# Weight loads of a hybrid encoder layer: issued from GpSimd's queue in place of SyncE's

## The chip, the core and the metric

The kernel runs on one core of a Trainium2 chip. TensorE multiplies matrices, VectorE and ScalarE do elementwise work, GpSimd can do some of it too, and SyncE (SP) computes nothing: it issues transfers. A transfer is issued by one engine's queue and then carried by the core's 16 DMA engines, which move it between the main memory and the on-chip memory; an engine that needs it waits for its landing. The metric is the device time in microseconds, lower is better. The kernel before took 2712.67 us (median of three runs, 2711.59 to 2713.68).

## What is computed

One layer of a bidirectional encoder, for a prompt of 1024 tokens and a sample of 2048, each with 16 learned meta tokens ahead, width 1024, in float32. One projection feeds two branches, which are gated, projected, merged and projected again:

```
xn = rmsnorm(h, g_pre)
proj = xn @ w_in + b_in                                  # 1024 -> 6672 columns
na_q, na_k, na_v, na_z, ml_qk, ml_v, ml_z, ml_o, ml_g, mg = split(proj)
ya = (neighbourhood_attention(na_q, na_k, na_v) * silu(na_z)) @ w_a
yb = (mlstm_bidirectional(ml_qk, ml_v, ml_g, ml_o) * silu(ml_z)) @ w_b
ga, gb = split(sigmoid(mg))
y = (ga * ya + gb * yb) @ w_out
out = h + rmsnorm(y, g_post)
```

## The kernel before

**Precision.** Every large product is made of three matmuls: a float32 operand is split into a high part (what the fast matmul format holds) and a low part (the rest), and hi*hi, hi*lo and lo*hi are added (`mm3`). So each weight tile exists twice on the chip, as `whi` and `wlo`, 128 x 1024 or 128 x 1056 numbers each, 512 or 528 KB.

**Where a weight comes from.** `requests` writes down at the start, in order, every weight unit that the dense work will take. A unit comes in one of three ways.
- Raw, the first time it is used: `wload` loads it from the input `wu` into `wraw` (L274); ScalarE copies it to `whi` (L303), VectorE takes the difference for `wlo` (L304), and both halves are written back to main memory to be kept (`wflush`, L331).
- Kept halves: later uses load `wh` and `wl` straight into `whi` and `wlo` (L296).
- Block sums: a part of the input projection uses a Strassen-like scheme with seven products for eight. Its sums of weight blocks are made on the side (`wprep`, `nprep`), stored as `q...`, and loaded in pairs into `whi` and `wlo` (L289).

**Buffers.** There are four `whi` and four `wlo` (`NBW = 4`) and two to four `wraw`. `wtake` hands a unit to the matmuls; `wdone` after a unit's last matmul is followed by `wpump`, which asks for the next load. On the chip that load waits until the buffer's last reader is through, and the matmuls wait until it has landed.

**The two streams.** `dense` runs the projections, the merges and the output products group by group in the order of `PLAN`; `sparse` runs the mLSTM and the attention. `run` weaves the two together by estimated costs. TensorE's order is the order in which this weave writes it down (`manual_schedule` holds TensorE alone). The order of the other engines' instructions, SyncE's and GpSimd's queues among them, is laid out when the program is built, by a simulation with estimated durations; each queue then runs strictly in that order, and an instruction whose wait isn't over holds up those behind it.

**The queues.** SyncE issues nearly every transfer: weights, tokens, the stores of the projections (`st`, `stT`) and their loads by the sparse stream (`raw`, `va`, `um`, `kf`, `tog`), the attention's operands, the kept halves, the gates `tg` and the output. GpSimd's queue holds 100 instructions: small memsets (among them the edges of `raw`, L1413 and L1415, and `st`, L1559), eight small copies, and 14 loads of constants for the attention, one-hot rows (L1096) and masks (L1183).

Of the kernel before, what the change touches and what calls it, by code (L numbers as in the profile page):

```python
# [10 lines left out]
F32 = mybir.dt.float32  # L11
# [126 lines left out]
class K:  # L138
# [127 lines left out]
    def wload(self, most=2):  # L266

        while self.wreq and sum(x[1] is not None for x in self.wraw) < most:
            key, src, nk, w = self.wreq.popleft()
            raw = None  # L270
            if key[0] != "q" and key not in self.wseen:
                self.wseen.add(key)
                raw = self.wrp[0].tile([P, 4 * WU], F32, name="wraw", bufs=self.wrp[1])
                self.nc.sync.dma_start(raw[:, :nk * w], src)  # L274
            self.wraw.append((key, raw, nk, w))

    def wpump(self, most=NBW, parts=1, copy=None):


        nc, wp = self.nc, self.wp  # L280
        self.wload()
        while self.wraw and self.wout < most:
            key, raw, nk, w = self.wraw.popleft()
            n = nk * w
            hi = wp.tile([P, 4 * WU], F32R, name="whi", bufs=NBW)
            lo = wp.tile([P, 4 * WU], F32R, name="wlo", bufs=NBW)
            if key[0] == "q":
                for x, k in zip((hi, lo), key[1:]):
                    nc.sync.dma_start(x[:, :n].bitcast(F32), self.qd[k][:, :])  # L289
                self.wrdy.append([x[:, :n].rearrange("p (h k c) -> p h k c", h=2, k=4) for x in (hi, lo)])  # L290
                self.wout += 1
                self.wload()
                continue
            if raw is None:
                for x, d in zip((hi, lo), self.wkept[key]):
                    nc.sync.dma_start(x[:, :n].bitcast(F32), d[:, :])  # L296
            else:
                for a in range(parts):
                    c = slice(a * n // parts, (a + 1) * n // parts)
                    if copy:  # L300
                        copy(hi[:, c], raw[:, c])
                    else:
                        nc.scalar.activation(hi[:, c], raw[:, c], AF.Copy)  # L303
                    nc.vector.tensor_tensor(lo[:, c], raw[:, c], hi[:, c].bitcast(F32), op=ALU.subtract)  # L304
                if key[1] in N_COLS and key[0] == "i":
                    j = N_COLS.index(key[1])
                    for a in range(2):
                        d = self.qd[j // 2, f"{j % 2 + 1}{a + 1}"] = self.dp.tile([P, D], F32, name=f"q{j}{a}")
                        for h, x in enumerate((hi, lo)):
                            self.hold.append((d[:, 512 * h:512 * h + 512], x[:, 512 * a:512 * a + 512].bitcast(F32)))  # L310
                else:
                    self.wkept[key] = []
                for x, part in ((hi, "h"), (lo, "l")) if key in self.wkept else ():
                    d = self.dp.tile([P, n], F32, name=f"w{part}{len(self.wkept)}")
                    self.hold.append((d, x[:, :n].bitcast(F32)))
                    self.wkept[key].append(d)
                if not self.early:
                    self.wflush()
                if key[0] in "mo":
                    self.wrdy.append(None)  # L320
                    self.wout += 1
                    self.wload()
                    continue
            self.wrdy.append([x[:, :n].rearrange("p (k c) -> p k c", k=nk) for x in (hi, lo)])
            self.wout += 1
            self.wload()
# [1836 lines left out]
```

## Time and profile before

| | |
|---|---|
| median of the runs | 2712.67 us |
| the profiled execution | 2707.9 us |
| its span, first to last instruction | 2706.1 us |
| instructions | 47482 |
| mean granted TensorE clock | 0.992 |
| moved by DMA | 805.75 MB, mean 298 GB/s |

The profile is of one execution. Its page gives the busy time of each engine (a matmul's end is modelled, so a busy TensorE need not run at its peak), the span in 40 slices, the DMA queues (q1 is SyncE's, q0 GpSimd's), and the chain of work that ended last, followed back from the end. Other views give the waits of one engine by what ended them, the busy time in chosen stretches, and the instructions of a queue in order of time. PE stands for TensorE, DVE for VectorE, ACT for ScalarE, POOL for GpSimd, SPq for SyncE's queue. L274 is line 274 of the kernel.

### The profile page before, as it was taken

The numbers are of one execution on the slowest core, as the hardware profiler recorded it, in microseconds if no ns is written. First come the engines' busy times: TensorE is split into PE (matmuls) and PEld (weight loads), VectorE is DVE, ScalarE is ACT, GpSimd is POOL, SyncE is SP. The second block draws the span as 40 slices with busy tenths as digits, with TensorE's granted clock in tenths as the row PEclk, the third lists the DMA queues.
The fourth block names the chain that finished last, engine by engine and source line by source line (L and its number), as shares of the span: only waits on it lengthen the run. The fifth ranks groups of instructions, "written<-read, shape, count | busy, mean of one in ns | idle before, by whom it ended". The sixth has DMA issues, their size and how long they took to land.

```text
span 2706.1 us, 47482 instructions
## 1 busy us (share of the span) xinstructions
PE 2647.0 (98%) x15928; PEld 2336.6 (86%) x15928; DVE 1943.8 (72%) x5266; ACT 1439.9 (53%) x3388; POOL 16.2 (1%) x100
## 2 busy tenths in 40 slices
PE   9999899998999999999999999999999999999998
PEld 7998798898987999887888888888889998989888
DVE  5655588787766888545686776867478989898954
ACT  5433456554444655555665566656365666656521
POOL 0000000000000000000000000000000000000000
PEclk9999899998999999999999999999999999999999
DMA  9899886899978899878889998899899898898965
GB/s 366 336 342 335 309 306 233 299 336 327 348 228 285 294 320 314 274 265 276 259 271 332 370 297 264 279 331 363 274 305 314 259 309 278 282 305 260 324 238 203
DMA packets 411651, 805.75 MB, mean 298 GB/s; under 512 B 52016, under 2 KB 180992, under 8 KB 409104
## 3 DMA queue, kind: packets, MB, share of 16 engines
q1 hardware_dynamic: 410288, 800.04, 87.9%
q0 software_dynamic: 1120, 2.69, 0.4%
q8 instruction: 126, 2.06, 0.3%
q14 instruction: 117, 0.96, 0.1%
HBM read 548.96 MB, written 253.60 MB: 297 GB/s over the span
## 4 chain that ended last, share of the span: by engine, by line
PE 82%; DMA 9%; DVE 5%; ACT 2%; issue 1%; SPq 1%; DVEq 0%; ACTq 0%
PE pj L202 9%; PE pj L204 9%; PE pj L203 9%; PE pj L971 7%; PE pj L973 7%; PE pj L972 7%; PE pj L776 4%; PE pj L777 4%; PE pj L778 4%; PE pj L1918 3%; PE pj L1919 3%; PE pj L1920 3%; PE sm L1266 3%; PE tr L1251 2%; DMA wraw<-wu 2%
## 5 line engine op out<-in xcount | busy, mean ns | idle before, releaser
L202 PE MATMUL pj<-xh,whi 128*128 128x512 f32 (+1 forms) x896 | 345.5, 386 | 1.0 <-ACT whi L303 0.9
L204 PE MATMUL pj<-xh,wlo 128*128 128x512 f32 (+1 forms) x896 | 337.4, 377 | 5.7 <-DMA wlo<-wl 5.4
L203 PE MATMUL pj<-xl,whi 128*128 128x512 f32 (+1 forms) x896 | 337.9, 377 | 0.1
L776 PE MATMUL pj<-whi,xh 128*128 128x256 f32 (+1 forms) x1152 | 330.9, 287 | 6.8 <-DMA whi<-wh 6.8
L777 PE MATMUL pj<-wlo,xh 128*128 128x256 f32 (+1 forms) x1152 | 326.2, 283 | 3.7 <-DMA wlo<-wl 3.7
L778 PE MATMUL pj<-whi,xl 128*128 128x256 f32 (+1 forms) x1152 | 325.9, 283 | 0.0
L776 PEld LDWEIGHTS pj<-whi,xh 128*128 128x128 f32 x1152 | 218.6, 190 | 7.4 <-DMA whi<-wh 7.0
L777 PEld LDWEIGHTS pj<-wlo,xh 128*128 128x128 f32 x1152 | 218.3, 190 | 4.1 <-DMA wlo<-wl 4.0
L1918 PE MATMUL pj<-whi,mh 128*128 128x256 f32 x768 | 219.8, 286 | 0.5 <-DMA whi<-wh 0.5
L778 PEld LDWEIGHTS pj<-whi,xl 128*128 128x128 f32 x1152 | 218.3, 189 | 0.0
L1920 PE MATMUL pj<-whi,mlo 128*128 128x256 f32 x768 | 216.6, 282 | 0.0
L1919 PE MATMUL pj<-wlo,mh 128*128 128x256 f32 x768 | 216.6, 282 | 0.0
L204 PEld LDWEIGHTS pj<-xh,wlo 128*128 128x128 f32 x896 | 170.9, 191 | 38.8 <-DMA wlo<-wl 6.2
L202 PEld LDWEIGHTS pj<-xh,whi 128*128 128x128 f32 x896 | 170.9, 191 | 30.8 <-ACT whi L303 1.8
L203 PEld LDWEIGHTS pj<-xl,whi 128*128 128x128 f32 x896 | 170.9, 191 | 27.5 <-issue 1.0
L1258 DVE TENSOR_TENSOR pts<-tr,pts 96x384 fp32r<-96x384 f32 (+2 forms) x192 | 118.5, 617 | 57.2 <-ACT pts L1253 55.3
L1253 ACT ACTIVATE pts<-tr 96x384 fp32r<-96x384 f32 (+2 forms) x192 | 103.5, 539 | 98.8 <-PE tr L1251 98.1
L202 PE MATMUL pj<-yh,whi 128*128 128x512 f32 x384 | 154.4, 402 | 0.0
L203 PE MATMUL pj<-yl,whi 128*128 128x512 f32 x384 | 150.9, 393 | 0.8 <-DVE yl L1820 0.8
L204 PE MATMUL pj<-yh,wlo 128*128 128x512 f32 x384 | 151.1, 394 | 0.0
L1918 PEld LDWEIGHTS pj<-whi,mh 128*128 128x128 f32 x768 | 145.4, 189 | 1.5 <-DMA whi<-wh 0.7
L1919 PEld LDWEIGHTS pj<-wlo,mh 128*128 128x128 f32 x768 | 145.5, 189 | 0.8
(368 smaller groups left out, 6962.5 us busy)
## 6 DMA issues: line engine op xcount, KB each, us to landing
whi<-wh SPq DMA_DIRECT2D x136, 512.0 KB
wlo<-wl SPq DMA_DIRECT2D x136, 512.0 KB
whi<-q SPq DMA_DIRECT2D x62, 512.0 KB
wlo<-q SPq DMA_DIRECT2D x50, 512.0 KB
wraw<-wu SPq DMA_DIRECT2D x48, 512.0 KB
gt<-st SPq DMA_DIRECT2D x96, 256.0 KB
tg<-gt SPq DMA_DIRECT2D x96, 256.0 KB
wh<-whi SPq DMA_DIRECT2D x36, 512.0 KB
```

Of the source, the lines that this page charges most:

```text
L202: mm(out, ah, bh, start=start, stop=False)
L203: mm(out, ah, bl, start=False, stop=False)
L204: mm(out, al, bh, start=False, stop=stop)
L776: nc.tensor.matmul(o, xh, wh, start=k == 0, stop=False)
L777: nc.tensor.matmul(o, xh, wl, start=False, stop=False)
L778: nc.tensor.matmul(o, xl, wh, start=False, stop=k == KT - 1)
L971: mm(bank, w[:, 0, k], xh[:, k], start=fresh and k == 0, stop=False, skip_group_check=True)
L972: mm(bank, w[:, 0, k], xl[:, k], start=False, stop=False, skip_group_check=True)
L973: mm(bank, w[:, 1, k], xh[:, k], start=False, stop=k == 3, skip_group_check=True)
L1918: nc.tensor.matmul(o, mh[:, k, xs], wh, start=clear > 0 and k == 0, stop=False)
L1919: nc.tensor.matmul(o, mh[:, k, xs], wl, start=False, stop=False)
L1920: nc.tensor.matmul(o, ml[:, k, xs], wh, start=False, stop=clear < 2 and k == KT - 1)
```

## The change

The three places in which the kernel loads weights issue from GpSimd instead of SyncE. Sources, destinations, sizes, buffers and the order of requests in the code stay.

```diff
@@ wload @@
-                self.nc.sync.dma_start(raw[:, :nk * w], src)
+                self.nc.gpsimd.dma_start(raw[:, :nk * w], src)
@@ wpump @@
             if key[0] == "q":
                 for x, k in zip((hi, lo), key[1:]):
-                    nc.sync.dma_start(x[:, :n].bitcast(F32), self.qd[k][:, :])
+                    nc.gpsimd.dma_start(x[:, :n].bitcast(F32), self.qd[k][:, :])
...
             if raw is None:
                 for x, d in zip((hi, lo), self.wkept[key]):
-                    nc.sync.dma_start(x[:, :n].bitcast(F32), d[:, :])
+                    nc.gpsimd.dma_start(x[:, :n].bitcast(F32), d[:, :])
```

The write-back of the halves (L331), the loads of raw weights for the block sums (L576, L608) and everything else stay with SyncE.

## The prediction

> **What bounds the kernel now.** I read the page first, then TensorE's own waits, then the stretches in which it waits, then the queue that issues the loads.
>
> ```profile
> span 2706.1 us, 47482 instructions
> PE 2647.0 (98%) x15928; PEld 2336.6 (86%) x15928; DVE 1943.8 (72%) x5266; ACT 1439.9 (53%) x3388; POOL 16.2 (1%) x100
> ...
> DMA  9899886899978899878889998899899898898965
> ...
> q1 hardware_dynamic: 410288, 800.04, 87.9%
> q0 software_dynamic: 1120, 2.69, 0.4%
> ...
> PE 82%; DMA 9%; DVE 5%; ACT 2%; issue 1%; SPq 1%; DVEq 0%; ACTq 0%
> ```
>
> TensorE is the bound: busy 2647.0 of 2706.1 us, so all its idle time together is 59.1 us and nothing done to loads can win much more than that. The second thing to see is the DMA row: the 16 DMA engines are nearly full almost everywhere. GpSimd is free (16.2 us busy).
>
> TensorE's waits say how much of the 59.1 us belongs to weights:
>
> ```profile
> PE tr L1539 <- DVE kf L1503: 11.7, 2, 8.9
> PE pj L776 <- DMA whi<-wh: 6.8, 1, 6.8
> PE sm L204 <- DVE ktl L1543: 6.4, 6, 2.8
> PE pj L204 <- DMA wlo<-wl: 5.4, 2, 2.8
> ...
> PE pj L777 <- DMA wlo<-wl: 3.7, 1, 3.7
> ...
> PE pj L202 <- ACT whi L303: 0.9, 1, 0.9
> ...
> PE pj L1918 <- DMA whi<-wh: 0.5, 1, 0.5
> ```
>
> (Total us, times, longest.) Waits for a weight load's landing: 6.8 + 5.4 + 3.7 + 0.5 = 16.4 us, in five events. They cost more than their idle time, as the stretches around them show (the number after POOL's count is the granted TensorE clock, then DMA share and GB/s):
>
> ```profile
> 630.60:642.00 11.40, 0.91 (x5) 0.41 (x3) 1.23 (x2) 0.80 (x3) 0.00 (x0) 0.65 1.01 344
> 642.00:648.00 6.00, 6.00 (x29) 6.00 (x30) 1.99 (x7) 2.60 (x6) 0.00 (x0) 0.52 1.02 368
> 754.00:766.00 12.00, 9.47 (x35) 7.21 (x35) 5.74 (x19) 4.64 (x14) 0.00 (x0) 0.86 0.85 268
> 812.00:824.00 12.00, 9.17 (x32) 6.55 (x31) 3.77 (x16) 1.86 (x4) 0.00 (x0) 0.86 1.03 404
> 900.00:1000.00 100.00, 99.23 (x775) 96.75 (x774) 80.75 (x197) 57.42 (x123) 0.00 (x0) 1.00 1.00 332
> 1500.00:1600.00 100.00, 98.57 (x505) 83.03 (x504) 79.02 (x292) 62.46 (x169) 0.20 (x2) 1.00 0.99 344
> 1800.00:1900.00 100.00, 96.92 (x483) 80.28 (x483) 70.04 (x236) 57.44 (x157) 0.10 (x1) 1.00 1.00 365
> ```
>
> After the stall that ends at 642 TensorE is busy without a gap for 6 us at a granted clock of 0.52: 6 x 0.48 = 2.9 us lost. The stalls near 760 and 817 lose 12 x 0.14 = 1.7 us each. So the weight stalls cost 16.4 + 6.3 = 22.7 us.
>
> Why are those loads late? SyncE's issues before the stall at 760, and pieces of the chain of waits (start, length from issue to landing):
>
> ```profile
> 749.84 0.42 SPq L296 DMA_DIRECT2D whi<-wh  x1
> 750.42 3.92 SPq L835 DMA_DIRECT2D nv<-stT  x6
> 755.36 0.33 SPq L296 DMA_DIRECT2D wlo<-wl  x1
> ...
> 758.19 0.39 SPq L296 DMA_DIRECT2D whi<-wh  x1
> ```
>
> ```profile
> 635.84 6.11 DMA wlo<-wl
> ...
> 755.36 4.79 DMA wlo<-wl
> ...
> 803.13 14.04 DMA wlo<-wl
> ```
>
> The two halves of one weight are 5.5 us apart, because six stores of nv stand between them in SyncE's order. The load itself then took only 4.79 us: it was issued late. The third one, issued at 803.13, took 14.04 us: it was slow, with DMA at 1.03 of its share in that stretch.
>
> SyncE also waits for transfers that its next load doesn't need, and its order is met late where an engine is late:
>
> ```profile
> SPq L2007 <- DVE yo L2006: 40.5, 28, 10.8
> ...
> SPq L1603 <- DMA yb<-szg: 25.9, 12, 3.8
> ```
>
> **The change part by part.** Moved are the raw loads at L274, the block sums at L289 and the kept halves at L296:
>
> ```profile
> L274 SPq DMA_DIRECT2D wraw<-wu x52: 328/494/1561, 2.6 to 946.7; - x52
> ...
> L296 SPq DMA_DIRECT2D whi<-wh x144: 319/378/1519, 461.5 to 2674.3; - x144
> L296 SPq DMA_DIRECT2D wlo<-wl x144: 319/370/1559, 465.3 to 2673.9; - x144
> ```
>
> With the 120 pairs of block sums that the order of the Strassen-like products asks for in the code, that is 52 + 288 + 240 = 580 loads of 512 or 528 KB, about 300 MB of the 800.04 MB. No byte, matmul or wait for data is added; TensorE's order is fixed by hand.
>
> *Loads no longer stand behind stores.* This removes the stalls at 637, 642 and 760, and the 0.5 us. The stall at 817 was a slow transfer in a full stretch; a queue of its own may or may not help, so I count half of its 2.7 + 1.7 us. Sum: 22.7 - 2.2 = **-20.5 us**; bounds 0 and -22.7.
>
> *The price of an issue on GpSimd and the landing.* The trace has no weight load there; the nearest row is the masks' load, 64 partitions of up to 4 KB instead of 128:
>
> ```profile
> L1183 POOL DMA_DIRECT2D kx<-masks x10: 509/513/779, 802.6 to 2423.7; - x10
> ...
> DMA to landing us min/median/max: 3.3/6.7/9.8
> ```
>
> At 0.513 us, 580 issues are 298 us of GpSimd, spread over the span; if the price goes with partitions, 595 us. Both lie beside TensorE. A pair takes 1.0 to 2.1 us. How much time is there? In the last stage loads are issued one weight apart:
>
> ```profile
> 2668.14 0.32 SPq L296 DMA_DIRECT2D wlo<-wl  x1
> ...
> 2673.88 0.32 SPq L296 DMA_DIRECT2D wlo<-wl  x1
> ```
>
> 5.74 us per weight; four buffers, so a load that goes out when its buffer comes free has three more weights ahead of it, 17.2 us. Less 1.0 for the pair and 6.7 for landing, 9.5 us are left; with the largest values (2.1, 9.8), 5.3. So this costs nothing, except where fewer weights are ahead, at the very end, where the row L1918 waits already: I take **+0.3** (2 x 0.513 against 0.32 + 0.38 of the issues there), at most +5.0 (9.8 against 4.79 to land).
>
> The Trainium skill, "SBUF — State Buffer", section "SBUF: two separate sides", speaks against the change: GpSimd writes descriptors through a port pair that VectorE locks in its two-port modes; its next section gives a transfer of about 0.62 us that then took about 3.1. By that page, an estimate of 2.5 us per load would leave 7.0 of the 9.5 us, and the sum would rise only at the end of the kernel, by 2.5. By the row, the ten mask issues stayed within 509 to 779 ns though VectorE was 72% busy; I go by the row.
>
> *Loads now stand behind GpSimd's own instructions.* Those wait long:
>
> ```profile
> POOL kx L1183 <- PE sm L1220: 720.6, 6, 297.0
> POOL raw L1413 <- DVE cv L1428: 273.2, 5, 74.9
> ```
>
> Most of that is GpSimd with nothing else to do. The order on each queue is laid out at build time by estimated times, so a load is late only by what an engine is late against the estimate. SyncE's order is made in the same way, and its longest wait for an engine is 10.8 us (L2007); 9.5 us are covered, 1.3 not. I take **+1**; lower bound 0, upper bound in the rivals.
>
> *SyncE is freed* of 580 issues at about 0.37 us, 215 us, and of waiting for weight buffers. The waits of TensorE for kf and ktl (11.7 and 6.4) end on VectorE, whose inputs come over that queue; I take **-1**, bounds 0 and -18.1. *The order on VectorE, ScalarE and SyncE* is laid out anew with it, and TensorE's waits for them could shrink or grow: **+2**, bounds -10 and +15, the latter near all that TensorE now waits for kf and ktl.
>
> Sum: -20.5 + 0.3 + 1 - 1 + 2 = -18.2 us. The profiled execution took 2707.9 us (span 2706.1 and 1.8 around it), so 2689.7; the median of the runs is 4.8 above that execution, so the forecast is 2712.67 - 18.2 = **2694.5**.
>
> **The rivals.**
>
> *The stalls stay (about 2711).* For it: in three of the four stall rows the DMA share is over 1.00, so the load may be slow on any queue, as the one of 14.04 us was. Against it: 749.84 to 755.36 is pure order, at a share of 0.85. The half hidden gain of one late pair leaves 2.7 + 1.7 at 760 and little else.
> The Trainium skill, "DMA: Bandwidth & Descriptors", section "Issuing engines are not separate DMA queues", says that more issuing engines save issue time alone, which would be this rival.
>
> *Slower: GpSimd's transfers cost the DMA engines more.* q0 uses 0.4 points for 2.69 MB, 0.149 per MB; q1 87.9 for 800.04, 0.110. That is 1.35 times (1.18 to 1.52 with the rounding of 0.4). The moved bytes are 38% of all, so a stretch at full share gets 0.38 x 0.35 = 13% longer. Over the three stretches above, +40 us, with the gain 2694.5 + 40 = 2734. It decides from 0.38 x 300 x excess = 18 us, a price 16% up. Against it: half of q0's loads are under 4 KB per row and write 64 partitions, and their times hold waiting for others.
>
> *Slower: GpSimd's order holds loads up.* A memset of raw or a mask load whose partner is late by more than 9.5 us stops all four buffers; each event costs about 3 us and 1.7 of clock. Four of them eat the gain; ten, +47, give 2741. For it: waits of 75 and 297 us stand in the rows. Against it: SyncE's 10.8.
>
> *Slower: the new order.* Taken at +33 in place of +2 (TensorE's waits for kf and ktl tripled): 2726.
>
> **How the numbers follow.** Under 0.2% (5.4 us) nothing can be told from no change. Forecast 0.56, its own range 2672 (all weight stalls and the kf and ktl waits gone) to 2707; stalls stay 0.14; dearer transfers 0.12; GpSimd's order 0.12; new order 0.06. Faster: 0.53 of the forecast and 0.04 of the stay, 0.57. Same: 0.03, 0.10 and 0.01 each of the two slow rivals, 0.15. Slower: 0.28. The range cuts the lower end where kf's wait, VectorE's own work, would have to go too, and holds the first two slow rivals' low part: 2678 to 2735.
>
> **What would show it.** Right: no wait of TensorE for whi or wlo near 640 and 760, clock 1.00 there, GpSimd's issues at 0.5 to 1.1 us, its landings under 10 us. Wrong: TensorE waiting for whi or wlo in new places with a GpSimd instruction in front (its order), DMA share at 1.00 over most slices with fewer GB/s (dearer transfers), or the same stalls under GpSimd's queue (they stay).

## The result: slower, and the profile after

| | before | after |
|---|---|---|
| median of the runs | 2712.78 us | 2734.36 us |
| lowest to highest | 2711.59 to 2713.68 | 2731.27 to 2736.21 |
| profiled execution, its span | 2707.9, 2706.1 us | 2731.3, 2729.5 us |

The ratio is 1.0079, 95% interval 1.0061 to 1.0096: 21.6 us slower, where the prediction said 18.2 faster. (The kernel before ran once more beside the change, so its median is 2712.78 here.) The page of the kernel after, first its busy times, the DMA row, the two queues, the chain's shares by engine and two rows of DMA issues (the last number is the median from issue to landing):

```profile
span 2729.5 us, 47658 instructions
PE 2653.3 (97%) x15928; PEld 2338.2 (86%) x15928; DVE 1940.8 (71%) x5266; ACT 1440.7 (53%) x3388; POOL 325.9 (12%) x680
...
DMA  9889986799968999988899998898989898898965
...
q1 hardware_dynamic: 326768, 495.58, 54.2%
q0 software_dynamic: 84640, 307.14, 33.7%
...
PE 76%; DMA 14%; DVE 5%; ACT 2%; issue 1%; SPq 1%; DVEq 0%; POOL 0%; ACTq 0%
...
whi<-wh POOLq DMA_DIRECT2D x136, 512.0 KB, 7.3
wlo<-wl POOLq DMA_DIRECT2D x136, 512.0 KB, 7.7
```

The change did what it says: 304 MB went over to q0. TensorE has the same 15928 matmuls in the same order; it was busy 6.3 us longer (its mean granted clock was 0.990 in place of 0.992) and idle 76.2 us in place of 59.1, together the 23.4 us by which the span grew. The two queues' shares are 54.2 + 33.7 = 87.9 and were 87.9 + 0.4. The chain's part in DMA rose from 9 to 14%. TensorE's waits say which transfers these are:

```profile
PE tr L1539 <- DVE kf L1503: 11.1, 2, 6.6
PE sm L204 <- DVE ktl L1543: 9.2, 6, 5.4
PE pj L203 <- DMA xl<-xl: 7.4, 2, 4.1
PE pj L971 <- ACT pj L1010: 6.6, 2, 5.6
PE sc L1668 <- DVE q L1622: 5.6, 1, 5.6
...
PE pj L202 <- ACT xh L389: 2.9, 1, 2.9
...
PE pj L1918 <- DMA whi<-wh: 1.2, 1, 1.2
```

Of the 16.4 us of waits for weights 1.2 are left. The new waits are for tiles that SyncE still loads, or that VectorE and ScalarE make from them.

One place shows how. There both kernels' SyncE reaches the same four loads of 1 MB (`xl`, `xh`, L936) at the same time, 1457.6 us. SyncE's issues (start, length) before:

```profile
1457.61 0.37 SPq L936 DMA_DIRECT2D xl<-xl  x1
1458.07 2.66 SPq L936 DMA_DIRECT2D xh<-xh  x2
1460.78 1.10 SPq L936 DMA_DIRECT2D xl<-xl  x1
1461.93 2.73 SPq L289 DMA_DIRECT2D whi<-q  x1
```

and after, on SyncE and then on GpSimd:

```profile
1457.67 0.37 SPq L936 DMA_DIRECT2D xl<-xl  x1
1458.13 1.44 SPq L936 DMA_DIRECT2D xh<-xh  x2
1459.62 6.71 SPq L936 DMA_DIRECT2D xl<-xl  x1
1466.42 2.31 SPq L712 DMA_DIRECT2D gt<-st  x1
```

```profile
1458.16 0.53 POOL L289 DMA_DIRECT2D whi<-q  x1 [2.46 <-PE sm L203]
1461.88 0.53 POOL L289 DMA_DIRECT2D wlo<-q  x1 [3.18 <-PE pj L973]
```

Before, the next weight stood behind the fourth of these loads. After, two weights set out among them. What both queues moved in the 20 us from 1457.6, before and then after (packets, MB, share of the 16 engines):

```profile
DMA packets 4007, 7.39 MB, mean 369 GB/s; under 512 B 265, under 2 KB 1247, under 8 KB 4006
q1 hardware_dynamic: 4006, 7.37, 103.3%
```

```profile
DMA packets 3111, 7.23 MB, mean 362 GB/s; under 512 B 178, under 2 KB 434, under 8 KB 3110
q1 hardware_dynamic: 2312, 4.27, 64.1%
q0 software_dynamic: 798, 2.94, 38.8%
```

The sum hardly changes; SyncE's queue gets 4.27 MB of it. Before, weights were among its 7.37 MB too, but the four loads came first. In the chain of waits of the kernel after (start, us from issue to landing) that fourth load is the longest transfer; it and two more of the long ones:

```profile
1459.62 23.24 DMA xl<-xl
1534.77 17.31 DMA xh<-t0h
1809.39 17.12 DMA kf<-kf
```

By its semaphore's update in the trace the same load took 12.4 us before (1460.78 to 1473.22).

### The profile page after: what moved, and what is told of

Read it like the earlier page. It is cut to its first block, busy times and chain, and to the rows that moved or that the text cites. A ratio compares the mean times of both kernels' runs of the same rounds, so it can differ in the third digit from the quotient of the medians.

```text
span 2729.5 us, 47658 instructions
## 1 busy us (share of the span) xinstructions
PE 2653.3 (97%) x15928; PEld 2338.2 (86%) x15928; DVE 1940.8 (71%) x5266; ACT 1440.7 (53%) x3388; POOL 325.9 (12%) x680
## 3 DMA queue, kind: packets, MB, share of 16 engines
q1 hardware_dynamic: 326768, 495.58, 54.2%
q0 software_dynamic: 84640, 307.14, 33.7%
## 4 chain that ended last, share of the span: by engine, by line
PE 76%; DMA 14%; DVE 5%; ACT 2%; issue 1%; SPq 1%; DVEq 0%; POOL 0%; ACTq 0%
PE pj L202 8%; PE pj L203 8%; PE pj L204 8%; PE pj L971 7%; PE pj L973 7%; PE pj L972 7%; PE pj L776 4%; PE pj L778 4%; PE pj L777 4%; PE pj L1918 3%; PE pj L1919 3%; PE pj L1920 3%; PE sm L1266 2%; PE tr L1251 2%; DMA stk<-nq 2%
## 5 line engine op out<-in xcount | busy, mean ns | idle before, releaser
L1918 PE MATMUL pj<-whi,mh 128*128 128x256 f32 x768 | 219.2, 285 | 1.2 <-DMA whi<-wh 1.2
L1918 PEld LDWEIGHTS pj<-whi,mh 128*128 128x128 f32 x768 | 145.1, 189 | 2.2 <-DMA whi<-wh 1.4
```

Source lines behind the costliest of these rows:

```text
L1918: nc.tensor.matmul(o, mh[:, k, xs], wh, start=clear > 0 and k == 0, stop=False)
```

## The experiments

Three theories. **S**, sharing: the 16 DMA engines serve both queues at once, so weights that have time to spare take turns from SyncE's loads that have none. **O**, order: the build lays out the other engines' instructions anew, and that order is worse. **D**, dearer: GpSimd's issues or transfers cost more in themselves.

To tell O apart, most kernels here hold VectorE, ScalarE and SyncE to the exact order of the kernel before, with order-only links between neighbours on an engine that make no engine wait for another. The loads that change queue (`off`) are left out of the links:

```diff
+        row = [row[n] for n in order]
+        for a, b in zip(row, row[1:]):
+            tc.add_manual_dep(b, a.name, info, reason="pin")
...
-        K(tc, ins, outs).run(ctx)
+        k = K(tc, ins, outs)
+        k.run(ctx)
+        pin(tc, k.off)
```

Line numbers in their profiles lie 1 to 6 higher. As TensorE's order is the same in all kernels, the n-th matmul of one trace can be put beside the n-th of the kernel before, and the difference of their starts is TensorE's lag. The table under e13 gives how much the lag grew in each stretch.

**e1: all weights on GpSimd, every other order as before.**

```diff
-                self.nc.sync.dma_start(raw[:, :nk * w], src)
+                self.off.add(self.nc.gpsimd.dma_start(raw[:, :nk * w], src).ins.name)
...
```

(and the same at L289 and L296)

> Weights on GpSimd as in the change, but the instructions of VectorE, ScalarE and SyncE (its other transfers) are held in exactly the order that they have in the kernel before. Theory S (sharing: a queue of its own gives the weight loads, which have time, an equal turn at the 16 DMA engines with SyncE's loads, which have none): the loss stays, 2728 to 2740 us, with no wait of TensorE for whi or wlo over 1 us but waits that end on SyncE's loads. Theory O (order: the build laid out the other engines anew and worse): the loss goes and the weight stalls' 20 us come in, 2690 to 2707 us. Theory D (GpSimd's transfers or issues cost more in themselves): as S, 2728 to 2740.

Measured: 2741.84, ratio 1.0110 (1.0089 to 1.0131): 1.8 us over the range that S and D share, and far from O's. The longest wait for a weight's landing is 1.2 us, at the kernel's end; at the opening TensorE waits 3.0 us for a raw weight's split on ScalarE, which S did not name.

**e2: the weights back on SyncE, the other engines in the order of the changed kernel.**

> The mirror image: weights back on SyncE, in the order that the build of the change gives to VectorE, ScalarE and SyncE's other transfers. S and D: near the kernel before, 2706 to 2722 us. O: as slow as the change, 2728 to 2740 us.

Measured: 2714.81, ratio 1.0009 (0.9998 to 1.0020). The loss is there without the new order, and the new order without the queue has no loss that can be measured. O falls.

**e3: as e1, each load in two halves of its columns, to make packets half as long.**

```diff
-                    nc.sync.dma_start(x[:, :n].bitcast(F32), d[:, :])
+                    for c in range(2):
+                        c = slice(c * n // 2, (c + 1) * n // 2)
+                        self.off.add(nc.gpsimd.dma_start(x[:, c].bitcast(F32), d[:, c]).ins.name)
```

> As the first, but each weight load is cut into two of half the columns, so rows of 2 KB in place of 4 KB and 1160 issues on GpSimd in place of 580. S, if turns are taken by packet: the weights' share falls, SyncE's loads land sooner (tg's median, 8.4 us in the change, under 7.8), 2715 to 2728 us. O: the same as the first run within 3 us. D: dearer, over 2738 us.

Measured: 2745.94, ratio 1.0116 (1.0093 to 1.0140). It didn't test what it was made for: q0 still shows 71808 packets of 4096 bytes, two rows of 2 KB in each. As a test of D it says something: its time is in D's range (over 2738), but so is e1's, and 580 more issues than e1 moved the ratio from 1.0110 to 1.0116, well inside the intervals.

**e4, e6, e7: one kind of load alone on GpSimd**, the 52 raw ones (L274), the 288 kept halves (L296), the 240 block sums (L289).

> Only the 52 raw loads on GpSimd, all other orders as before. S: the start loses what it lost in the change (TensorE's start held up by xt, some 4 to 8 us) and little else, 2714 to 2724 us. O: at or under the kernel before, 2700 to 2713. D: 52 issues cost next to nothing, 2711 to 2716.

> Only the 288 loads of kept halves on GpSimd (most of them issued at 400 to 1100 us and from 1950 on), the other 292 on SyncE, the order of VectorE, ScalarE and SyncE that of before. Theory S: only those steps of e1 remain at whose time kept halves are under way: +6 at 482, -11.5 at 638, +6 at 669 to 690, -7 at 760 to 821, +6.5 at 1034 to 1079, +7 at 1958 to 2050; none at the opening nor at 1269 to 1815. Sum about +7: 2714 to 2726. Theory D: each load costs its share wherever it is, 288/580 of the losses of e1 (about 48) less the gains (18): 2712 to 2724 as well, but with small steps also after 2050, where e1 showed none.

> Only the 240 loads of block sums on GpSimd (all issued at 1100 to 1950 us), the other 340 on SyncE, the order of VectorE, ScalarE and SyncE that of before. Theory S: only the losses of e1 at 1269 to 1302 (5.8), 1478 (5.7), 1815 (6.7) and part of 1958 (up to 4.4) remain, and the stalls for weights of before at 638 to 821 come back, so that no gain is left: 2728 to 2738, slower than before by about 20. Theory D: 240/580 of the losses: as much, but spread over the stretch and not at these four places.

Measured: 2719.16, ratio 1.0024 (1.0012 to 1.0037); 2719.66, 1.0021 (1.0009 to 1.0033); 2734.26, 1.0081 (1.0065 to 1.0096). The three add up to 1.26%, near e1's 1.10%. e4's time is in S's range and above those of O and D, and it lost 5.1 us at the opening, as S named; e6's is in both S's and D's. e7's is in S's range, and it lost at places that S named (6.1 us near 1478, 3.4 at 1815, 7.0 near 1958) and at one that it didn't (3.5 at 1873), while 1302 stayed small; it is flat after 1970. Its 3.8 us at 1000 to 1110 come before its first moved load (1126 us); e4 shows 3.6 there after its last (953 us). e6 has the gains, and steps at 482, 650 to 715 and 1034 to 1079, but only 2.1 of the 7 us that S put at 1958 to 2050. It also lost 6.0 us after 2200, where e1 lost 0.8; S has no step there, and D's many small ones don't fit either: most of it is one, at 2226. The trace shows there a load of SyncE's (`vr`) that took 15.5 us (9.0 before), and a wait of 3.5 us for what is made from it: the kind of step that S means, at a place that it did not name.

**e5: as e1, but 524 loads of weights wait until the SyncE load that stood just ahead of them before has landed.**

```diff
+    for i, j in json.loads(zlib.decompress(base64.b85decode(AFTER))):
+        tc.add_manual_dep(w[i], sp[j].name, info, reason="after")
```

(here the link is a wait for the landing; `w` are the weights' loads, `sp` SyncE's)

> All 580 loads of weights on GpSimd and VectorE, ScalarE and SyncE held to the order of the kernel before, as in e1, with one thing added: 524 of the 580 loads of weights wait until the one load of SyncE's that stood just ahead of them in the kernel before has landed (the other 56, whose tile would by the trace of before be late by it, don't wait). So a load of weights no longer shares the 16 DMA engines with the loads that were issued ahead of it. By the landings of before this starts a weight 3.3 us later in the median, and none of the 524 lands under 3 us ahead of its first use. Theory S (the weights' own queue takes turns from SyncE's tight loads): the losses of e1 against before (TensorE fell back by 2.9 us at 7 to 14, 6.2 at 482, 6.2 at 669 to 690, 6.5 at 1034 to 1079, 5.8 at 1269 to 1302, 5.7 at 1478, 6.7 at 1815, 7.2 at 1958 to 2050) go in the main, and the gain at 638 to 646 and 760 to 821 (-18) stays: 2690 to 2718. Theory D (an issue or a transfer by GpSimd is dearer or disturbs SyncE's queue in itself): the waits take no issue and no transfer away, so 2735 to 2755.

Measured: 2720.90, ratio 1.0032 (1.0019 to 1.0044). With every one of GpSimd's 580 issues still made, 21 of e1's 30 us are gone. D can't explain that; S had it at 2718 at most, so a little is missing. Two places say why. One is that of the four loads: e5's DMA in the 20 us from their first issue, and the issue of the fourth:

```profile
q1 hardware_dynamic: 2029, 3.84, 52.2%
q0 software_dynamic: 1008, 3.67, 48.3%
```

```profile
1448.95 5.54 SPq L937 DMA_DIRECT2D xl<-xl  x1
```

Here the waits only pushed weights back from the loads ahead into these four: q0 moved 3.67 MB beside them, more than in the changed kernel, and this step stayed (4.4 us). The other lies after 2200, where e5 fell back by 8.3 us and e1 by 0.8: there TensorE waits for weights that GpSimd issued late, two of them after pauses of 14 and 15 us (e1's longest between 2190 and 2500 is 8.1).

```profile
PE pj L1919 <- DMA whi<-wh: 4.5, 3, 2.2
PE pj L1920 <- DMA wlo<-wl: 1.8, 2, 0.9
```

**e8, e10, e11: other tenants for GpSimd's queue.** In e8 542 stores move to it (`st`, `stT`, kept halves), weights stay on SyncE and nothing is held. In e10 the tight loads move, `kf` (L1585), `um` (L1591), `va` (L1476), `raw` (L1416) and `xl`, `xh` (L936); in e11 only `kf`, `um`, `xl`, `xh`; VectorE and ScalarE are held.

```diff
-        nc.sync.dma_start(um, src)
+        self.off.add(nc.gpsimd.dma_start(um, src).ins.name)
```

> The opposite way to give SyncE's queue room: the weights stay on SyncE and 542 stores of SBUF tiles to DRAM (kept halves, features, keys, gates, values) are issued by GpSimd; nothing is held, so the order of the other engines may change a little. Theory S: stores on a queue of their own take turns from the tight loads as well, while SyncE's loads no longer stand behind stores that wait for their data; both signs: 2700 to 2735, and the transfers of xl, kf, um are longer while a store is under way. Theory D: 542 issues by GpSimd against 580 in the change: slower by about 20.

> The mirror image: the weights stay on SyncE, and 368 loads that TensorE, VectorE or ScalarE use soon after they land (kf, um, va, the raw keys and queries, and xl and xh of L936) are issued by GpSimd; VectorE and ScalarE are held to the order of before, SyncE's order may change. Theory S: now these loads take their turns beside the queue of weights and stores instead of standing behind it, and land earlier, while the weights have 16.5 us to spare in the median: 2688 to 2714. If both queues share alike whoever is in them, but GpSimd's order holds a load up behind another's buffer: up to 2730. Theory D (GpSimd's loads are dearer in themselves): 368/580 of e1's 48 us of losses, and on loads without slack: 2735 to 2760.

> As e10 with 160 loads only: kf (L1585), um (L1591), and xl and xh of L936 on GpSimd; va and the raw keys and queries stay on SyncE. Theory S: the steps of e1 at 669 to 690, 1269 to 1302, 1478 and 1815 were these tiles, so most of e10's gain is in these: 2692 to 2714. Theory D: 160/580 of 48 us on loads without slack: 2722 to 2735.

Measured: e8 2724.20, ratio 1.0039 (1.0026 to 1.0052); e10 2727.57, 1.0060 (1.0046 to 1.0073); e11 2711.74, 0.9995 (0.9984 to 1.0007). e8 lost 6.0 us at 1440 to 1520 without a weight on GpSimd, but not at the four loads: by its semaphore the fourth landed 14.2 us after its issue (12.4 before), and TensorE did not wait for it. It waited 2.8 us for keys made from `kf`, which took 12.7 us to land (8.2 before). In those 13 us GpSimd's stores moved 0.79 MB and SyncE's queue 4.39; as SyncE's order is not held in e8, this fits S without showing it. e8's time is in S's wide range; of the 20 us that D gave it, it lost 11. e10 missed S's gain and came near the end that S gave to GpSimd's order; D's 2735 and more is missed too, and e11 missed D's 2722 by far; it is inside S's range, without a gain that can be measured. What GpSimd waited for in e10, issuing one load behind another's buffer:

```profile
POOL um L1592 <- DVE sl L1689: 82.4, 23, 7.8
POOL va L1477 <- DVE den L1718: 68.5, 16, 5.3
```

That this is what cost e10 its gain was not tried by itself. A queue of their own didn't bring the tight loads in sooner, as S had expected of it: `um` took 5.3 us to land in the median before and 6.2 in e11.

**e12: the block sums of e7 on ScalarE's queue instead.**

```diff
-                    nc.sync.dma_start(x[:, :n].bitcast(F32), self.qd[k][:, :])
+                    self.off.add(nc.scalar.dma_start(x[:, :n].bitcast(F32), self.qd[k][:, :]).ins.name)
```

> The 240 loads of block sums of e7 on ScalarE's queue, a second hardware queue, and none of the weights on GpSimd; VectorE and SyncE held to the order of before, ScalarE too but for the place of the loads between its instructions. Theory S as it stands (any second queue takes turns from SyncE's): the losses of e7 come back at the same places (1302, 1478, 1800 to 1815, 1873, 1958), 2728 to 2745, where the upper end holds what ScalarE's own time for the issues adds (its later instructions behind loads that wait for their buffer). If only a queue that GpSimd feeds does it (its descriptors are made by software): none at these places, 2711 to 2720, plus what ScalarE's time for the issues costs, which would stand as waits of TensorE for ScalarE and not for tiles that SyncE loads.

Measured: 2750.13, ratio 1.0129 (1.0101 to 1.0157), above both. The waits of TensorE that grew:

```profile
PE sm L203 <- ACT kth L1543: 17.0, 5, 7.0
PE pj L972 <- ACT pj L989: 5.8, 3, 3.5
```

They end on ScalarE, whose own work stands behind loads that wait for buffers. What both queues moved in the 20 us from the first of the four loads (q10 is ScalarE's):

```profile
q1 hardware_dynamic: 3325, 5.40, 76.7%
q10 hardware_dynamic: 492, 1.76, 25.8%
```

So this hardware queue takes a share at once as well, and by its semaphore the fourth load took 16.7 us, where it had taken 12.4. How much of the loss is this and how much ScalarE's own time stays open; the run mixes the two.

**e13: as e1, but four loads of weights wait for the fourth of the four loads near 1478.** In e1 these pairs landed 18 to 20 us ahead of their use.

> e1 (all weights on GpSimd, other orders as before) with one difference: four loads of weights near 1470 to 1480 us (the pairs of the two units that in e1 were under way while xl and xh of L936 were loaded, and that in e1 landed 18 to 20 us ahead of their use) wait until the last of these four loads of SyncE's has landed. Theory S: the last xl lands some 12 us after its issue as in the kernel before, and not 23 as in e1; TensorE's step of 5.7 us at 1478 of before's time goes (0 to 1.5 left), every other step stays as in e1, and the time is 2733 to 2740. Theory D, or any cost of GpSimd's issues that isn't the shared transfer: the step stays at 5 to 6, since as many issues are made; 2739 to 2746.

Measured: 2740.31 in its one run, 0.3 us above S's range and inside D's, so the time decides nothing; the step does. Chain and wait at that place in e1, and then in e13:

```profile
1471.33 22.66 DMA xl<-xl
```

```profile
PE pj L204 <- DMA xl<-xl: 3.5, 1, 3.5
```

```profile
1467.03 14.75 DMA xl<-xl
1482.84 7.99 DMA wlo<-q
```

```profile
PE pj L203 <- DMA wlo<-q: 2.0, 1, 2.0
```

The same load landed in 14.7 us in place of 22.7, and TensorE no longer waits for it. Nothing but four weights was moved out of its way: here the cause of the step is shown. They were held a little too long (2.0 us of wait for `wlo`, which is most of the 2.5 us that this stretch still loses). Another 4.9 us came back at 1520 to 1770, most of it in a wait of 3.3 us for `xh`; that the freed weights caused this is not shown. Other steps differ from e1's by up to 4 us: the step is S's, the "every other step stays" is not.

How much TensorE's lag against the kernel before grew, in us, by stretches of the kernel before:

| stretch | after | e1 | e5 | e7 | e9 | e13 |
|---|---|---|---|---|---|---|
| 0 to 48 (`xt`, raw weights) | +5.2 | +4.7 | +3.1 | +0.2 | -0.1 | +4.6 |
| 400 to 540 | +4.3 | +6.3 | +2.8 | 0.0 | 0.0 | +5.1 |
| 625 to 650 (weight stalls) | -13.8 | -13.8 | -13.8 | -2.1 | -13.8 | -13.8 |
| 650 to 715 (`ktl`) | +4.9 | +8.0 | +7.9 | -1.4 | +8.9 | +7.3 |
| 715 to 790 (weight stall, `q`) | +5.2 | -3.0 | -4.5 | +0.7 | -4.5 | -2.5 |
| 790 to 850 (weight stall) | -4.7 | -4.7 | -4.7 | +0.4 | -4.7 | -4.7 |
| 1000 to 1110 (`stk`) | +0.1 | +8.7 | +3.2 | +3.8 | +0.2 | +9.2 |
| 1110 to 1440 | -0.5 | +6.7 | -2.5 | +0.9 | 0.0 | +3.4 |
| 1440 to 1520 (the four loads) | +6.5 | +5.8 | +4.4 | +6.1 | 0.0 | +2.5 |
| 1520 to 1770 | -1.0 | 0.0 | +0.7 | +1.0 | 0.0 | +4.9 |
| 1770 to 1860 | +6.4 | +7.3 | +4.7 | +3.4 | +1.8 | +2.9 |
| 1860 to 1920 | 0.0 | 0.0 | 0.0 | +3.5 | 0.0 | +3.7 |
| 1920 to 2070 | +10.2 | +7.4 | 0.0 | +7.0 | 0.0 | +8.7 |
| 2200 to the end | +2.1 | +0.8 | +8.3 | +0.2 | +0.4 | +3.0 |
| whole | +24.0 | +33.3 | +7.1 | +24.1 | -11.3 | +33.0 |

The stretches left out are under 2 us each. These are steps of one execution (e5's took 2714.4 us, 6.5 under its median). One of under some 4 us says little by itself: at 1000 to 1110 e2, e4 and e7 lost 3.6 to 4.6 with none of the moved loads under way.

**e9: six loads only.** The prediction's gain alone: the three pairs of halves that TensorE waited for in the kernel before go to GpSimd, 574 loads stay.

```diff
+                    d = d[:, :]
+                    if self.nkept in LATE:
+                        self.off.add(nc.gpsimd.dma_start(x[:, :n].bitcast(F32), d).ins.name)
+                    else:
+                        nc.sync.dma_start(x[:, :n].bitcast(F32), d)
+                    self.nkept += 1
```

> Six loads of kept halves on GpSimd, those of the three units that TensorE waited for at 638 to 646, 757 to 760 and 817 in the kernel before (of 580 loads only these stood 8 to 34 us behind SyncE's other work after their buffer was free); the other 574 on SyncE, the order of VectorE, ScalarE and SyncE that of before. The term of the prediction (stalls for weights, with the clock after them) says -20; what e5 showed behind them, where hardly a load of weights shared (TensorE fell back 8.1 us between 663 and 694, at a tile of keys that came no earlier than before), says that 5 to 9 of it are given back at once. Both theories expect no sharing to speak of from six loads: theory S 2697 to 2707, nothing moved at the opening, at 482, at 1034 to 1079, at 1269 and after. If the stalls were not SyncE's order: 2711 to 2716.

Measured: **2696.92**, ratio 0.9947 (0.9935 to 0.9959), 0.1 us outside the expected range and the fastest of all. Its page's span, and TensorE's waits:

```profile
span 2694.4 us, 47498 instructions
```

```profile
PE tr L1545 <- DVE kf L1509: 11.7, 2, 8.9
PE sm L205 <- DVE ktl L1549: 9.9, 9, 2.8
...
PE pj L1924 <- DMA whi<-wh: 0.5, 1, 0.5
```

The weight stalls are gone and no new wait for `xl`, `stk` or `q` has come. 8.9 us of the gain are lost again between 650 and 715, where TensorE now waits 3.0 us for `ktl` and 2.5 for `v`; in all, `ktl` rose from 6.4 to 9.9.

## Why the prediction was wrong

The measured 2734.4 us lie just inside the range of 2678 to 2735, but by luck: its upper end stood for dearer transfers and for GpSimd's order, and neither was seen.

*Loads no longer stand behind stores, -20.5: right.* The steps of the table (e9's column) are -13.8, -4.5 and -4.7, together 23.0, against 22.7 worked out for all of the stalls. Even the one of 14.04 us went, which the prediction had counted half. But it did not ask what is late next: in e9 8.9 us of it come back at once, at `ktl` and `v`. The rival that the stalls stay (2711) is not seen.

*Issue and landing on GpSimd, +0.3: right.* The wait at the kernel's end (L1918) rose from 0.5 to 1.2 us. Weights' loads in the trace of after (busy us, mean ns of one | idle before):

```profile
L296 POOL DMA_DIRECT2D whi<-wh x144 | 77.1, 535 | 484.2 <-PE pj L204 360.9 <-DMA wh<-whi 62.8 <-PE pj L778 23.4
L296 POOL DMA_DIRECT2D wlo<-wl x144 | 77.0, 534 | 486.6 <-PE pj L1920 237.5 <-PE pj L778 150.1 <-DMA wl<-wlo 44.1
```

128 partitions cost 0.53 us, as 64 did (0.51), not twice. Landings of 7.3 and 7.7 us in place of 6.7 leave 8.5 of the 9.5 us of slack. The Trainium skill's rule that VectorE locks GpSimd out ("SBUF — State Buffer", "SBUF: two separate sides") did not show in the issues: the longest on GpSimd took 0.89 us, at a VectorE that is 71% busy, where the prediction's estimate from that page was 2.5 more per load. How much of VectorE's work ran in such modes no view here says.

*Loads behind GpSimd's own instructions, +1, and its rival (2741): not seen.* The waits for weights are 1.2 us.

*The new order, +2: right as a term; its rival (2726): not seen.* e2 puts it at +2.6 with an interval that reaches zero.

*Dearer transfers (2734): not seen.* The rival named nearly the time measured, but the two queues' shares add up to 87.9%, against 88.3 before, where it would have had them rise. After the change q0 uses 33.7 points for 307.14 MB, 0.110 per MB, and q1 54.2 for 495.58, 0.109; the 1.35 times came from a row of 2.69 MB and does not hold for these loads.

**"SyncE is freed", -1, with bounds 0 and -18.1: the step that failed.** The term asked how SyncE's loads would gain from 580 fewer issues and let them lose nothing. In fact they lost: after against before the lag grew by 24.0 with 23.0 of stalls gone, so 47 us came back, 8.9 of which e9 shows too, without sharing to speak of. That leaves some 38 us for this term, in place of -1 (with a few of the new order in it); e1, with the order of before, leaves 47 by the same sum. That the cause is the weights under way at the same time is shown at the four loads (e13) and, for the loss as a whole, by e5, where waits alone take 21 of e1's 30 us away; place by place it was not tried elsewhere. The row that should have warned was quoted: the DMA row at 9 nearly everywhere. In a resource that is full, a load that starts sooner makes another land later; the weights, which by an estimate from the trace of before had 16.5 us to spare in the median (from landing to first use), moved ahead of loads with none. SyncE's one queue had been their order of urgency.

A rule by which this would come about stands in the Trainium skill, "DMA: Bandwidth & Descriptors", section "Queues, rings and completion order": each DMA engine goes round the queues that have work and takes a packet from each in turn. The traces agree as far as they show it (64.1 and 38.8% at once, the weights landing in 6.5 us, in the median of those 20 us, beside 4 MB of SyncE's); turns of equal size are not shown. The sentence that the prediction took from the same page, that more issuers only save issue time, does not hold here: with the orders held, e1 lost 1.1% and e9 won 0.5%.

## What to carry to other kernels

In this kernel, whose DMA engines are nearly full, one queue worked as an order of priority: the four loads on SyncE's queue landed in the order of their issue, the last after 12.4 us. A second queue took its share at once (38.8% beside 64.1), however little its loads hurried. Before moving a class of transfers, list the slack of what stays, not only of what moves, and move the few that are late (six here: -0.5%) instead of the class (580: +0.8%). And ask of each stall removed which tile is the next one late.

## What was not expected of the hardware

SyncE itself was held up: the issue of the fourth load took 6.71 us after, 6.03 in e1 and 5.54 in e5, against 1.10 before (where no issue of SyncE's took over 3.54), and everything behind it in its order waited with it. What sets this length was not tried. And two rows of 2 KB went as one packet of 4096 bytes in e3, so cutting a load by columns didn't cut its packets.
